# A two-branch mixer block: recurrence units that hold two pairs of heads over 256 tokens, and a GpSimd queue in written order under the attention

## The chip, the cores and the metric

One core of one Trainium2 chip. The metric is the device time of one execution in microseconds (us); of several runs the median is taken.

## What is computed

One block with 1024 tokens of width 1024, all in fp32: a modulated RMS norm, a mixer of two branches (causal attention with a forget gate, 8 heads of 64; a delta-rule recurrence, 8 heads of 64), a gated merge, an output projection, and a feed-forward part with a short convolution. The change touches the two branches only:

```python
# recurrence, one step per token and head; state is 64 x 64
sa = einsum('bhvk,bhk->bhv', state, a_t)
state = state * w_t[:, :, None, :] + sa[..., None] * b_t[:, :, None, :] + v_t[..., None] * k_t[:, :, None, :]
y_t = einsum('bhvk,bhk->bhv', state, r_t)
# attention, per block of 128 queries
logits = einsum('bhqd,bhkd->bhqk', q, k) * scale + cum_q - cum_k     # cum: sums of the log forget gates
probs = softmax(where(causal, logits, -inf))
out = einsum('bhqk,bhkd->bhqd', probs, v)
```

## The kernel before, in words

**Order of the work.** TensorE's instructions stand in an order that the program writes itself (`manual_schedule`, L139). A planner, `Weave` (L48), keeps a model time `now`, advanced by a modelled cost for each matmul (`mm_cost`, L67). Work that has latency runs as chains (Python generators); a chain yields the time after which it wants to go on. While no chain is due, `fill` (L104) lets the next matmuls of a queue of projections run: items of `weave.first`, then of `weave.queue`. An item in progress is finished first, and one further item has had its weights loaded already, so a new item in `weave.first` starts behind both. An item that sets `weave.hold` stops the filling until that time. Except where a part of the program is marked as written order, the other engines' orders are made by a scheduler.

**Fill.** The projections of the recurrence's inputs `rkv_items` (L387; 24 halves of 24 matmuls of 128x512), of the attention's q and k (`qk_steps`, L400), of v (`v_steps`, L1032) and of 16 gates (`gate_steps`, L336; two halves of 24 matmuls each). Gates left at the attention's start run as its fill (`late_gate`, L1306, on the bank `rk_ps`), and what is left at its end runs behind it.

**Recurrence.** It is worked in chunks of 64 tokens. A unit is one pair of heads (128 rows: two heads of 64) over 512 tokens, that is 8 chunks; there are 4 pairs and 2 halves of the tokens, 8 units. Two chains run side by side:

- `pre` (L814) of unit k: decays, normalized keys and the scaled operands on VectorE and ScalarE (per-channel factors such as `V("k_k", p)` differ by pair); the chunks' matrices `E` by matmuls `p`; a round trip of their 32x32 blocks through DRAM (`sm`, `M32`) for `inverse` (L787), 62 small VectorE instructions, and back (`se`, `TT`); transposes and the bonus term. `ready` is the time at which the planner takes `TT` to have landed. `pre` of unit k waits until unit k-2 has passed two points of `main` (`passed`).
- `main` (L924) of unit k: VectorE transposes `X` out of `TT` (planned at `ready` less 1500 ns), then matmuls `xi`, `zi`, `uw`, `mz`, then the state's steps. A step per chunk: `sp` += Mt times S0 (one matmul for each of the two heads, each issued to TensorE as two instructions), VectorE scales it by the chunk's decay to the next state S (L996), `yp` += S0 times Zt. Between steps the chain yields 1150 ns, and the fill's matmuls come between. At the end come two head sums (`mu`, `va`), the normalization, and the store of the output to `d_orw`.

The tiles for r, k and v have one buffer for each half of the tokens; the items for the next pair are put into `weave.first` when `pre` of a unit is done, and `pre_chain` (L1058) runs the fill itself until a unit's inputs are there.

**Attention.** Three chains: logits (`s_chain`, L1122), transposes of the probabilities (`t_chain`, L1208), products with v (`a_chain`, L1251). VectorE and ScalarE are in written order here (L1109), GpSimd is not. GpSimd issues the loads of each head (`load_head`, L1093: `stA` of 1 MB, `stB` of 0.5 MB, `vh` of 0.5 MB, two buffers each), multiplies the outputs by the inverse sums and splits them into `fx` (`collect`, L1271). The inverse sums go through DRAM: ScalarE issues the store `d_rs` and, 3.5 us of plan later, the load `R` that spreads them over 64 rows (`spread`, L1194). The outputs' tile `o` has two buffers. ScalarE's table for Exp and Tanh is asked for at L1340, the table for Ln and Exp in `use_ln_exp` (L203).

Of the kernel before, what the change touches and what calls it, by code (L numbers as in the profile page):

```python
# [16 lines left out]
S = 1024  # L17
# [17 lines left out]
NVEC = _n  # L35
NOSYNC = mybir.DependencyInfo(mybir.DependencyClass.NoSync, mybir.DependencyReason.DATA)
# [99 lines left out]
def hybrid_block(ctx: ExitStack, tc: tile.TileContext, a, out):  # L136
# [66 lines left out]
    def use_ln_exp(after=None):  # L203

        i = nc.scalar.preload_act_table_set("natural_log_exp_and_others")
        if after is not None:
            tc.add_manual_dep(i.ins, after.ins.name, NOSYNC)
# [128 lines left out]
    def gate_steps(w, i, pps, ptag, pool, tag):  # L336
        if weave.late == 1:
            yield from late_gate(w, i)
            return
        for hf in range(2):  # L340
            cs = slice(hf * NH, hf * NH + NH)
            ps = pps.tile([128, NH], F32, tag=ptag, name=f"gt{i}_{hf}")
            yield from gemm_steps(ps, w[0:2], u, cs)

            g = pool.tile([128, NH], F32, tag=tag, name=f"gs{i}_{hf}")
            if weave.late:
                nc.scalar.activation(g, ps, AF.Tanh, scale=0.5)
# [6 lines left out]
            stt(g, ps, 0.0, g, op0=ALU.min, op1=ALU.subtract)  # L354
            nc.scalar.activation(g, g, AF.Exp)
            nc.sync.dma_start(d_gate[i, :, cs], g)
# [3 lines left out]
    with ExitStack() as es:  # L360
# [26 lines left out]
        def rkv_items(p, hf):  # L387
            ts_ = {x: rkp.tile([128, NH], F32, tag=f"{x}{hf}", name=f"{x}{p}{hf}") for x in "rkv"}
            rkv[p, hf], got[p, hf] = [ts_[x] for x in "rkv"], 0

            def steps(w, x, t):
                if hf == 0:
                    last_col[p, x] = shp.tile([128, 1], F32, tag=f"pv{x}", name=f"pv{p}{x}")
                yield from shifted(w, t, hf, ts_[x], last_col[p, x], f"rkv{t}")
                got[p, hf] += 1

            for x, t in (("k", 4 + p), ("r", p), ("v", 8 + p)):
                yield (lambda t=t: w_in(12 + t)), (lambda w, x=x, t=t: steps(w, x, t))
# [253 lines left out]
        with tc.tile_pool(name="lg", bufs=1, reuse_waits="tile") as lg, \  # L652
# [47 lines left out]
            def lora_chain():  # L700
# [11 lines left out]
                while got[0, 0] < 3:  # L712
                    weave.step()
# [48 lines left out]
            weave.first.extend([*rkv_items(0, 0), *rkv_items(0, 1)])  # L762
# [7 lines left out]
        def hx(ap, x):  # L770
            return ap.rearrange("p (c x) -> p c x", x=x)

# [14 lines left out]
        def inverse(n, M32, TT, chunk_tile, tmp):  # L787
# [3 lines left out]
            t32 = tmp("t32", 256)  # L791
# [22 lines left out]
        def pre(k, p, hf):  # L814

            n = f"{p}_{hf}"
            cs = slice(hf * NH, hf * NH + NH)
            rr, kk, vv = rkv[p, hf]
# [8 lines left out]
            nc.sync.dma_start(cum, d_lora[0, p, :, cs])  # L827
            al = tmp("al")
            nc.sync.dma_start(al, d_lora[1, p, :, cs])
            ksq = tmp("ksq")  # L830
            nc.scalar.activation(ksq, kk, AF.Square, scale=V("k_k", p))
            parts = rw.tile([128, 3, NH], F32R, tag="bk", name=f"kp{n}")
            yield 1275 if p + hf else 6000
# [12 lines left out]
            stt(kr, rn, 1e12, kk, op0=ALU.min, op1=ALU.mult)  # L846
# [4 lines left out]
            stt(ar[:, 0], c3(kr), nkk[:, p : p + 1], el[:, :, 0:CH], op0=ALU.mult, op1=ALU.mult)  # L851
# [3 lines left out]
            tt(ar[:, 1], c3(rr), el[:, :, 1:], op=ALU.mult)  # L855
            ts(al, al, V("k_a", p), oka[:, p : p + 1], op0=ALU.mult, op1=ALU.add)
            tt(al, al, kk, op=ALU.mult)
            tt(bk[:, :, 1, :], c3(al), c3(en), op=ALU.mult)
            pcd = chunk_tile("pcd", 3, NCU)
            nc.gpsimd.tensor_copy(pcd, el[:, :, CH])  # L860
            rkb = tmp("ksq")
            stt(rkb, rr, V("r_k", p), al, op0=ALU.mult, op1=ALU.mult)
# [26 lines left out]
            for g in range(4):  # L889
                nc.sync.dma_start(M32[g * 32 : g * 32 + 32, :, :], sm.rearrange("h c b s t -> (h c b) s t"))  # L890
            ready = weave.now + (47500 if k == 0 else 38500)
            TT = chunk_tile("TT", 2, NCU, CH)
            weave.spawn(inverse(n, M32, TT, chunk_tile, tmp), 8500)

            vt, at = gen(f"vt{n}"), gen(f"at{n}")
            for b in range(4):
                bs = slice(b * 128, b * 128 + 128)
                transpose(vt[:, bs], vv[:, bs], ident)
                transpose(at[:, bs], ar[:, 0, 2 * b : 2 * b + 2, :], ident)
# [21 lines left out]
            tt(bon, bp, vv, op=ALU.mult)  # L921
            units[p, hf] = dict(ready=ready, pcd=pcd, ar=ar, E=E, QA=QA, TT=TT, bon=bon, UV=UV)

        def main(k, p, hf):  # L924
            o = units.pop((p, hf))
            n = f"{p}_{hf}"
            cs = slice(hf * NH, hf * NH + NH)
# [52 lines left out]
            S0 = state.get(p)  # L980

            for c in range(NCU):
                alone = hf == 0 and c == 0
                for h in range(2):
                    mm(sp[HS[h], c, :], E[:, c, h, 2, :], UV[:, c, h, :], start=c == 0, stop=alone, more=True)
                for h in range(2):
                    mm(yp[HS[h], c, :], UV[:, c, h, :], E[:, c, h, 1, :], start=c == 0, stop=alone, more=True)
            yield 2400
            for c in range(NCU):
                if S0 is not None:  # L990
                    for h in range(2):
                        mm(sp[HS[h], c, :], Mt[HS[h], c, :], S0[HS[h], :], start=False, stop=True, more=True)
                S1 = None
                if not (hf == 1 and c == NCU - 1):
                    S1 = rw.tile([128, CH], F32, tag="state", name=f"S{n}{c}", bufs=3)
                    ts(S1, sp[:, c, :], pcd[:, c : c + 1], None, op0=ALU.mult)  # L996
                if S0 is not None:
                    for h in range(2):
                        mm(yp[HS[h], c, :], S0[HS[h], :], Zt[HS[h], c, :], start=False, stop=True, more=True)
                if c + 1 < NCU:  # L1000
                    yield 1150
                S0 = state[p] = S1
# [19 lines left out]
            nc.scalar.activation(rs, rs, AF.Exp, scale=-0.5)  # L1022
            stt(y, y, V("ln_w", p), rs, op0=ALU.mult, op1=ALU.mult)
            stt(y, y, V("ln_b", p), bon, op0=ALU.add, op1=ALU.add)
            gg = rw.tile([128, NH], F32, tag="Wt", name=f"gg{n}", bufs=1)
            nc.sync.dma_start(gg, d_lora[2, p, :, cs])
            ov = rw.tile([128, NH], F32, tag="ysq", name=f"o{n}", bufs=1)
            tt(ov, y, gg, op=ALU.mult)
            nc.sync.dma_start(d_orw[p, :, cs], ov)
# [25 lines left out]
        order = [(p, hf) for p in range(4) for hf in range(2)]  # L1055
        passed.update((k, x) for k in (-1, -2) for x in range(2))

        def pre_chain():  # L1058
            for k, (p, hf) in enumerate(order):
                while got[p, hf] < 3:  # L1060
                    weave.step()
                yield from pre(k, p, hf)
                if p < 3:
                    weave.first.extend(rkv_items(p + 1, hf))
                yield 0

        def main_chain():
            for k, (p, hf) in enumerate(order):
                while (p, hf) not in units:
                    yield 200  # L1070
                yield from main(k, p, hf)
# [11 lines left out]
    heads = {}  # L1083

    def load_first():
# [5 lines left out]
        heads[0] = *tiles[0:4], tiles[4].rearrange("p (a x) -> p a x", x=128)  # L1091

    def load_head(h):  # L1093
        A = at.tile([128, 2, S], F32R, tag="stA", name=f"stA{h}")
        nc.gpsimd.dma_start(A, d_st[h, 0:2, :, :].rearrange("k r s -> r k s"))
        B = at.tile([128, 2, S], F32R, tag="stB", name=f"stB{h}")
        nc.gpsimd.dma_start(B[0:68, :, :], d_st[h, 2:4, 0:68, :].rearrange("k r s -> r k s"))
        vh = at.tile([128, 8, 128], F32R, tag="vh", name=f"vh{h}")
        nc.gpsimd.dma_start(vh, d_v[h])
        heads[h] = A[:, 0, :], A[:, 1, :], B[:, 0, :], B[:, 1, :], vh  # L1100

    load_first()
    while len(weave.queue) > 12:
# [5 lines left out]
    with tc.manual_schedule(engines={mybir.EngineType.DVE, mybir.EngineType.Activation}):  # L1109
# [12 lines left out]
        def s_chain():  # L1122

            yield 3500
            for k, (h, I) in enumerate(seq):
                if k % 4 == 1 and h < 7:
                    load_head(h + 1)
                qa, ka, qb, kb, _ = heads[h]
# [19 lines left out]
        def softmax(h, rows, lgt):  # L1148
# [17 lines left out]
            for i, n, nm, lg in part:  # L1166
                e = (at.tile([128, S], F32, tag="P", name=f"P{h}_{i}", bufs=4) if i > 3 else
# [26 lines left out]
        def spread(h, hf, tp):  # L1194
            p = h // 2
            rt = at.tile([4, 128], F32, tag="rt", name=f"rt{h}_{hf}", bufs=1)
# [7 lines left out]
            nc.scalar.dma_start(norms[p, hf][h % 2 * 64 : h % 2 * 64 + 64, :],  # L1204
# [45 lines left out]

        def a_chain():  # L1251

            for _ in range(8 * 10):
# [6 lines left out]
                vh = heads[h][4]  # L1260
# [5 lines left out]
                th_free.append(weave.now + 260)  # L1266
                if jj == I:
# [72 lines left out]
        nc.scalar.preload_act_table_set("exp_and_others")  # L1340
# [28 lines left out]
    def br_open(x, n):  # L1369
# [5 lines left out]
        nc.scalar.copy(hi, raw)  # L1375
# [9 lines left out]
    use_ln_exp(marks["gate"])  # L1385
# [754 lines left out]
```

## Time and profile before

| | |
|---|---|
| median of 3 runs | 1646.33 us (1641.17 to 1647.93) |
| the profiled execution | 1646.9 us, span 1645.1 us |
| mean granted TensorE clock | 0.991 |

| stretch (us from the span's start) | what runs there |
|---|---|
| 0 to 136 | norm, low-rank projections, modulation |
| 136 to 612 | the recurrence with its fill |
| 612 to 812 | the attention with its fill |
| 812 to 899 | the branches' output projections (`br`) |
| 899 to 1645 | output projection and feed-forward part |

How to read it: a busy row counts an engine's instructions, the column in brackets says what ended the idle time before an instruction and how long it was. Matmuls overlap, so the cost of one in a series is the distance from start to start and not its own duration. `f32 x8` at the end of a row of the timeline are eight instructions in a row that were merged.

### The profile page before, as it was taken

The numbers are of one execution on the slowest core, as the hardware profiler recorded it, in microseconds if no ns is written. First come the engines' busy times: TensorE is split into PE (matmuls) and PEld (weight loads), VectorE is DVE, ScalarE is ACT, GpSimd is POOL, SyncE is SP. The second block draws the span as 40 slices with busy tenths as digits, with TensorE's granted clock in tenths as the row PEclk, the third lists the DMA queues.
The fourth block names the chain that finished last, engine by engine and source line by source line (L and its number), as shares of the span: only waits on it lengthen the run. The fifth ranks groups of instructions, "written<-read, shape, count | busy, mean of one in ns | idle before, by whom it ended". The sixth has DMA issues, their size and how long they took to land.

```text
span 1645.1 us, 25963 instructions
## 1 busy us (share of the span) xinstructions
PE 1614.0 (98%) x9756; PEld 1327.9 (81%) x9756; DVE 1197.2 (73%) x2334; ACT 808.4 (49%) x1473; POOL 139.7 (8%) x169
## 2 busy tenths in 40 slices
PE   7999999999999999999999999999999999999998
PEld 5777877887887778788888888888888888888886
DVE  6875887887876636777579346887777777786677
ACT  7663434443455546676524135644444444555455
POOL 0011101211111020222132000000000000000000
PEclk8999999999999999999999999999999999999999
DMA  9587644543343236543487310242332232675363
GB/s 346 185 314 228 166 129 122 136 121 91 111 119 89 89 107 179 135 136 106 148 322 259 135 65 27 83 135 96 104 114 96 96 109 97 223 256 160 122 211 109
DMA packets 123902, 241.72 MB, mean 147 GB/s; under 512 B 39816, under 2 KB 48320, under 8 KB 123776
## 3 DMA queue, kind: packets, MB, share of 16 engines
q1 hardware_dynamic: 114944, 220.94, 41.3%
q0 software_dynamic: 7600, 17.25, 3.8%
q10 hardware_dynamic: 1232, 1.86, 0.4%
q8 instruction: 77, 1.26, 0.3%
q14 instruction: 49, 0.40, 0.1%
HBM read 174.43 MB, written 65.56 MB: 146 GB/s over the span
## 4 chain that ended last, share of the span: by engine, by line
PE 88%; DVE 6%; ACT 3%; DMA 1%; issue 1%; POOL 0%; SPq 0%; DVEq 0%; ACTq 0%; POOLq 0%
PE X L144 14%; PE D L144 13%; PE Y L144 6%; PE gt L144 6%; PE ps_rkv L144 6%; PE wo L144 5%; PE br L144 5%; PE rk_ps L144 4%; PE qk L144 4%; PE W L144 3%; PE v L144 3%; PE ov L144 2%; PE lg L144 2%; PE tp L151 2%; PE low L144 1%; PE sp L144 1%
## 5 line engine op out<-in xcount | busy, mean ns | idle before, releaser
L144 PE MATMUL D<-op,op 128*128 128x512 f32 x924 | 209.8, 389 | 0.0
L144 PEld LDWEIGHTS D<-op,op 128*128 128x128 f32 x924 | 173.3, 188 | 36.3 <-DVE op L1403 0.3
L144 PE MATMUL X<-T_m,S 128*128 128x512 f32 x440 | 107.3, 390 | 0.1
L144 PEld LDWEIGHTS X<-T_m,S 128*128 128x128 f32 x440 | 82.4, 188 | 18.2 <-ACT T_m L1828 0.6
L1402 ACT CAST op<-g 128x512 fp32r<-128x512 f32 x77 | 47.8, 621 | 73.0 <-PE D L144 48.1
L1403 DVE TENSOR_TENSOR op<-g,op 128x512 fp32r<-128x512 f32 x77 | 53.0, 688 | 41.3 <-ACT op L1402 41.3
L1639 DVE SCALAR_TENSOR_TENSOR c<-ab,vec,c 128x512 f32<-128x512 f32 x88 | 65.9, 749 | 19.5 <-ACT c L1642 17.9
L1603 DVE TENSOR_TENSOR S<-ur,S 128x512 fp32r<-128x512 f32 x66 | 45.5, 691 | 35.6 <-ACT S L1599 35.5
L1246 DVE TENSOR_TENSOR tl<-tp,th 128x512 fp32r<-128x512 f32 (+1 forms) x80 | 49.9, 633 | 28.0 <-ACT th L1238 24.5
L270 DVE TENSOR_TENSOR lo_in<-raw_in,hi_in 128x512 fp32r<-128x512 f32 x84 | 57.9, 728 | 15.9 <-PE gt L144 7.7
L1599 ACT CAST S<-ur 128x512 fp32r<-128x512 f32 x66 | 41.0, 622 | 55.6 <-DVE ur L1592 30.6
L1603 DVE TENSOR_TENSOR A<-ur,A 128x512 fp32r<-128x512 f32 x64 | 44.0, 688 | 30.9 <-ACT A L1599 30.7
L266 ACT CAST hi_in<-raw_in 128x1024 fp32r<-128x1024 f32 x42 | 43.9, 1048 | 45.2 <-PE ps_rkv L144 28.0
L144 PE MATMUL Y<-T_h,A 128*128 128x512 f32 x264 | 63.5, 389 | 0.0
L795 DVE TENSOR_TENSOR t<-E,M 128x60 f32<-128x60 f32 (+24 forms) x248 | 54.8, 221 | 11.8 <-DMA M<-sm 5.7
L144 PE MATMUL Y<-T_h,S 128*128 128x512 f32 x264 | 63.3, 389 | 0.0
L799 DVE TENSOR_TENSOR E<-E,t 128x60 f32<-128x60 f32 (+24 forms) x248 | 57.9, 234 | 5.8
L144 PE MATMUL X<-B_b,A 128*128 128x512 f32 x252 | 60.8, 390 | 0.0
L144 PE MATMUL W<-B_f,A 128*128 128x512 f32 x252 | 60.6, 389 | 0.0
L1238 ACT CAST th<-tp 128x512 fp32r<-128x512 f32 (+1 forms) x80 | 42.4, 542 | 33.7 <-PE tp L151 31.3
L144 PEld LDWEIGHTS Y<-T_h,A 128*128 128x128 f32 x264 | 49.5, 188 | 10.4
L144 PEld LDWEIGHTS Y<-T_h,S 128*128 128x128 f32 x264 | 49.5, 188 | 10.3
(494 smaller groups left out, 4071.6 us busy)
## 6 DMA issues: line engine op xcount, KB each, us to landing
raw_in<-in_w_in SPq DMA_DIRECT2D x50, 512.0 KB
wm<-in_w_mod SPq DMA_DIRECT2D x48, 512.0 KB
ur<-in_w_up SPq DMA_DIRECT2D x44, 512.0 KB
g<-d_g SPq DMA_DIRECT2D x35, 512.0 KB
d_g<-gs SPq DMA_DIRECT2D x44, 256.0 KB
d_g<-c SPq DMA_DIRECT2D x33, 256.0 KB
d_st<-qh SPq DMA_DIRECT2D x64, 128.0 KB
d_gate<-gs SPq DMA_DIRECT2D x32, 256.0 KB
```

The lines of the kernel that those rows point to most:

```text
L144: weave.last = nc.tensor.matmul(o, lhsT, rhs, start=start, stop=stop, skip_group_check=more)
L266: i = nc.scalar.copy(hi, raw)
L270: nc.vector.tensor_tensor(lo[:, c : c + NH], raw[:, c : c + NH], f32(hi[:, c : c + NH]), op=ALU.subtract)
L795: i = tt(tv, E32[:, 0:J, s : s + 1].to_broadcast([128, J, W]), M32[:, s : s + 1, s + 1 : 32].to_broadcast([128, J, W]), op=ALU.mult)
L799: tt(E32[:, 0:J, s + 1 : 32], E32[:, 0:J, s + 1 : 32], tv, op=ALU.add)
L1238: nc.scalar.copy(th[:, 0:w], tp[:, 0:w])
L1246: tt(tl[:, 0:w], tp[:, 0:w], f32(th[:, 0:w]), op=ALU.subtract)
L1402: nc.scalar.copy(hi, src)
L1403: tt(lo, src, f32(hi), op=ALU.subtract)
L1599: nc.scalar.copy(hi, src)
L1603: tt(lo, src, f32(hi), op=ALU.subtract)
L1639: stt(c, ab[:, x + hf * NH : x + hf * NH + NH], V("conv_w", 22 * x + i), c, op0=ALU.mult, op1=ALU.add)
```

## The change

The recurrence's unit becomes two pairs of heads (a group g, with j = 0, 1) over 256 tokens (a quarter), still 8 chunks in a unit and 8 units. Chunk 4*j + i of a unit is chunk i of pair j, so a unit has 4 steps of the state in place of 8, each for both pairs. Operations with per-channel factors are split into two of 256 columns. Loads and stores of `d_lora` and `d_orw` cover two pairs by 256 columns.

```diff
         def rkv_items(g, hf, x):
             def steps(w, p, t):
+                if p % 2 == 0:
+                    while x not in free:
+                        weave.hold = weave.now + 200
+                        yield
+                    free.remove(x)
+                    rkv[g, hf, x] = rkp.tile([128, 2, NH], F32, tag=x, name=f"{x}{g}{hf}")
...
-            stt(kr, kr, V("k_k", p), al, op0=ALU.mult, op1=ALU.mult)
+            for j, p in pairs:
+                stt(j2(kr)[:, j], j2(kr)[:, j], V("k_k", p), j2(al)[:, j], op0=ALU.mult, op1=ALU.mult)
...
-            ready = weave.now + (47500 if k == 0 else 38500)
+            ready = weave.now + (47500 if k == 0 else 50000)
...
+            if not odd and (g, hf) != (1, 1):
+                for x in "krv":
+                    weave.first.extend(rkv_items(*((g, 1) if hf == 0 else (g + 1, 0)), x))
+            yield from arrived("v")
...
-            for c in range(NCU):
+            for i in range(4):
                 if S0 is not None:
-                    for h in range(2):
-                        mm(sp[HS[h], c, :], Mt[HS[h], c, :], S0[HS[h], :], start=False, stop=True, more=True)
+                    for j in range(2):
+                        for h in range(2):
+                            mm(sp[HS[h], 4 * j + i, :], Mt[HS[h], 4 * j + i, :], S0[HS[h], j, :], start=False, stop=True, more=True)
...
-                    ts(S1, sp[:, c, :], pcd[:, c : c + 1], None, op0=ALU.mult)
+                    tt(S1, sp[:, i::4, :], pcd[:, i::4].unsqueeze(2).to_broadcast([128, 2, CH]), op=ALU.mult)
...
-                if c + 1 < NCU:
-                    yield 1150
+                if i < 3:
+                    yield 1300
```

The tiles for r, k and v now have one buffer each, of two pairs by 512 tokens; a name is in `free` again when `pre` of an odd quarter has read it for the last time. The items for the next 512 tokens are put into `weave.first` in `pre` of an even quarter, behind its matmuls `p`; `pre` itself waits for its inputs by `arrived`, which polls every 200 ns while the other chains go on, in place of the loop in `pre_chain` that ran the fill.

In the attention GpSimd is in written order too; heads' loads carry a wait for the last TensorE instruction that was written before them; `vh` is loaded apart from `stA` and `stB`; head 1 is loaded before the attention's start; the load `R` is issued by GpSimd in place of ScalarE; `o` has three buffers, `rt` two; the probabilities of the four longer rows have a tile each.

```diff
+    def fetch(dst, src):
+        i = nc.gpsimd.dma_start(dst, src)
+        tc.add_manual_dep(i.ins, weave.last.ins.name, SYNC)
...
-    with tc.manual_schedule(engines={mybir.EngineType.DVE, mybir.EngineType.Activation}):
+    with tc.manual_schedule(engines={mybir.EngineType.Pool, mybir.EngineType.DVE, mybir.EngineType.Activation}):
...
-                if k % 4 == 1 and h < 7:
-                    load_head(h + 1)
+                if k % 4 == 1 and 0 < h < 7:
+                    load_head(h + 1, fetch)
+                if k in (2, 4):
+                    load_v(k // 2)
...
-            nc.scalar.dma_start(norms[p, hf][h % 2 * 64 : h % 2 * 64 + 64, :],
+            nc.gpsimd.dma_start(norms[p, hf][h % 2 * 64 : h % 2 * 64 + 64, :],
...
+                ends[h] = ends.get(h, 0) + 1
+                if ends[h] == 10 and 0 < h < 6:
+                    load_v(h + 2)
...
-                halves[p, hf] = at.tile([128, NH], F32, tag="o", name=f"o{p}{hf}"), []
+                halves[p, hf] = at.tile([128, NH], F32, tag="o", name=f"o{p}{hf}", bufs=3), []
```

Both table loads get an order: the one for Exp and Tanh behind the last Exp of an early gate (`early`) and of the recurrence (`rs`), the one for Ln and Exp behind the last gate and a copy of a branch's weights (`hi`).

```diff
-        nc.scalar.preload_act_table_set("exp_and_others")
+        table = nc.scalar.preload_act_table_set("exp_and_others")
+        for x in ("early", "rs"):
+            tc.add_manual_dep(table.ins, marks[x].ins.name, NOSYNC)
...
-    use_ln_exp(marks["gate"])
+    use_ln_exp(marks["gate"], marks["hi"])
```

More of the change, by code (lines that the diff above doesn't have):

```diff
@@ L711, in lora_chain @@
                 mod_out(5)
-                while got[0, 0] < 3:
+                while min(got.get((0, 0, x), 0) for x in "krv") < 2:
                     weave.step()
@@ L979, in main @@
             sp = py.tile([128, NCU, CH], F32, tag="sp", name=f"sp{n}")
-            S0 = state.get(p)
+            S0 = state.get(g)
             for c in range(NCU):
-                alone = hf == 0 and c == 0
+                alone = quarter == 0 and c % 4 == 0
                 for h in range(2):
@@ L1053, in hybrid_block @@
             weave.add(lambda i=i: w_in(26 + i), lambda w, i=i: gate_steps(w, i, pb, "big", gsp, "sp0"))
-        order = [(p, hf) for p in range(4) for hf in range(2)]
+        order = [(g, quarter) for g in range(2) for quarter in range(4)]
         passed.update((k, x) for k in (-1, -2) for x in range(2))
         def pre_chain():
[L1059 to L1064, printed above, removed]
+            for k, o in enumerate(order):
+                yield from pre(k, *o)
                 yield 0
         def main_chain():
-            for k, (p, hf) in enumerate(order):
-                while (p, hf) not in units:
+            for k, o in enumerate(order):
+                while k not in units:
                     yield 200
-                yield from main(k, p, hf)
+                yield from main(k, *o)
                 yield 0
@@ L1249, in halve @@
             av_queue.append((t + 210, h, I, jj, th, tl))
+        ends = {}
         def a_chain():
```

157 lines of the change are left out of this document (97 added, 60 removed).

## The prediction

> **What bounds the kernel now.** I read the page first, then the busy times by stage, then what TensorE waited for.
>
> ```profile
> span 1645.1 us, 25963 instructions
> PE 1614.0 (98%) x9756; PEld 1327.9 (81%) x9756; DVE 1197.2 (73%) x2334; ACT 808.4 (49%) x1473; POOL 139.7 (8%) x169
> ```
>
> TensorE (PE) is busy for 1614.0 of 1645.1 us. The 31 us of gaps are all that a shorter wait anywhere could give back; more must come from matmuls that get cheaper. The stages that the change touches, and the one group of gaps in the attention that is of any size, by columns of length, PE, weight loads, VectorE (DVE), ScalarE (ACT), GpSimd (POOL) and the granted clock:
>
> ```profile
> 266.00:314.00 48.00, 47.62 (x478) 36.83 (x473) 40.51 (x116) 21.20 (x39) 8.85 (x11) 1.00 0.55 141
> 612.00:812.00 200.00, 193.23 (x1169) 169.34 (x1168) 142.09 (x273) 131.12 (x299) 44.05 (x60) 0.98 0.46 131
> 682.00:692.00 10.00, 6.94 (x24) 5.73 (x23) 4.52 (x8) 3.80 (x11) 1.23 (x2) 0.66 0.71 194
> ```
>
> ```profile
> PE lg L144 <- ACT P L1173: 3.9, 4, 3.1
> PE rk_ps L144 <- ACT gs L1325: 2.5, 4, 1.2
> PE sp L144 <- DVE S L996: 1.0, 3, 0.4
> ```
>
> The first row is one unit of the recurrence: 48 us, PE without gaps, VectorE 84% busy. The state's chain, eight steps one after the other, makes PE wait 1.0 us in all (third row of the waits), because the fill covers it. So a shorter chain by itself gives nothing; it only moves fill to a later place. In the attention PE idles 6.8 of 200 us, 3.1 of them in one place, where the clock falls as well (0.66 over 10 us).
>
> **The change part by part. 1. The state's steps.** The timeline of PE in the last unit shows one visit to the state between two stretches of fill; then the pace of fill alone; then a long series of matmuls of the same 64x64 shape; last, both groups over the whole recurrence.
>
> ```profile
> 586.81 0.33 PE L144 MATMUL sp<-S,Mt 64*64 64x64 f32 x4
> 586.98 0.28 PE L144 MATMUL yp<-Zt,S 64*64 64x64 f32 x4
> 587.19 1.65 PE L144 MATMUL gt<-u_hi,lo_in 128*128 128x512 f32 x6
> 588.77 0.33 PE L144 MATMUL sp<-S,Mt 64*64 64x64 f32 x4
> ```
> ```profile
> 605.72 1.98 PE L144 MATMUL gt<-u_lo,hi_in 128*128 128x512 f32 x8
> 607.53 1.98 PE L144 MATMUL gt<-u_hi,lo_in 128*128 128x512 f32 x8
> ```
> ```profile
> 313.40 1.15 PE L144 MATMUL q<-UV,E 64*64 64x64 f32 x32
> 314.47 0.69 PE L144 MATMUL xi<-X,E 32*32 32x32 f32 x32
> ```
> ```profile
> L144 PE MATMUL sp<-S,Mt 64*64 64x64 f32 x240 | 19.9, 242 | 1.3 <-DVE S L996 1.0
> L144 PE MATMUL yp<-Zt,S 64*64 64x64 f32 x240 | 17.0, 218 | 0.0
> ```
>
> From one visit to the next are 588.77 - 586.81 = 1.96 us. Six fill matmuls take 6 x (607.53 - 605.72)/8 = 6 x 0.226 = 1.36 us, so a visit of 8 small matmuls costs 0.60 us. In a series 32 of that shape take 314.47 - 313.40 = 1.07 us, 0.033 each, 0.27 for eight. The other 0.33 us is paid for each visit, for going from fill to the state and back. There are 240/4 = 60 visits (60 x 0.60 = 36 us; the groups show 19.9 + 17.0 = 36.9). The change makes them 30 (8 units of 4 steps, less the two first steps of the two groups, which have no state), of 16 matmuls each: the matmuls are the same 480. Saved are 30 x 0.33 = 9.9 us, and as PE is the bound with no gaps here, they come off the time.
>
> The Trainium skill ("TensorEngine Tiling (Array Packing)", Key Properties) says that changing the tiling mode, between 128x128 fill and 64x64 state work here, drains TensorE; by that rule the cost goes with the visits, as I have it. The same page (Instruction Overhead) says that each matmul carries about 60 cycles; by that rule the cost goes with the matmuls, none of which go, and this term would be 0. The rows speak for the first, 0.075 us for a matmul in a visit against 0.033 in a series.
>
> Bounds: 0, if all of the 0.60 goes with the matmuls, and 30 x 0.60 = 18, if none does; I take 9.9, which both rows give.
>
> **2. The stop in the attention at 685 us.** ACT, GpSimd and PE around it:
>
> ```profile
> 683.26 0.36 ACT L1277 COPY o<-ov 64x256 f32<-64x256 f32 x1 [4.65 <-POOL fx L1296]
> ```
> ```profile
> 677.53 1.43 POOL L1290 TENSOR_TENSOR o<-o,R 128x256 f32<-128x256 f32 x2 [2.71 <-DMA R<-d_rs]
> 679.58 0.76 POOL L1095 DMA_DIRECT2D stA<-d_st  x1
> 680.34 1.00 POOL L1097 DMA_DIRECT2D stB<-d_st  x1
> 681.36 1.87 POOL L1296 TENSOR_TENSOR fx<-o,fx 128x256 fp32r<-128x256 f32 x2
> ```
> ```profile
> 677.47 0.40 PE L144 MATMUL lg<-stB 68*128 68x512 f32 x1
> 677.71 0.40 PE L144 MATMUL lg<-stA 128*128 128x512 f32 x1
> 685.40 0.79 PE L144 MATMUL lg<-stA 128*128 128x512 f32 x1 [3.06 <-ACT P L1173]
> 685.99 0.63 PE L144 MATMUL lg<-stB 68*128 68x512 f32 x1
> 686.41 0.63 PE L144 MATMUL lg<-stA 128*128 128x512 f32 x1
> ```
>
> ACT wants a new `o`; both buffers are taken until GpSimd's last read (L1296), which stood behind the wait for `R` and two load issues. ACT, in written order, held the next Exp, and PE stopped for 3.06 us. Then a logits matmul takes 686.41 - 685.99 = 0.42 us where it took 677.71 - 677.47 = 0.24: the clock is down for about 6 us (685.4 to 691.4), which costs 6 x (1 - 0.24/0.42) = 2.6 us. A third `o` takes away the wait for the buffer; the loads' issues (1.8 us here) come at the plan's places. Gain 3.1 + 2.6 = 5.7 us; bounds 0 and, with all of the 6.8 us of gaps, 9.4. I take 5.7, since this one wait is named by its row.
>
> What is added: 14 issues of `R` move from ACT to GpSimd. By GpSimd's issue rows they cost 0.4 to 1.0 us each, 6 to 14 us beside 44 busy of 200; behind each stand the multiplications by `R`, the `fx` splits and the next loads, and for `fx` nobody waits before the next stage. The new wait of `stA` and `stB` for PE stops GpSimd until the planned place; behind it stand the same. I take 0 here and put the case that loads come late among the rivals. `vh` no longer sits behind `stB`.
>
> **3. The table load.**
>
> ```profile
> 618.14 0.63 ACT L355 ACTIVATE gs<-gs 128x512 f32<-128x512 f32 x1 [0.76 <-DVE gs L354]
> 621.64 1.01 ACT L1173 ACTIVATE P<-lg,nm 128x896 f32<-128x896 f32 x1 [2.87 <-DVE nm L1162]
> 622.76 1.28 ACT L1325 ACT_TABLE_LOAD   x1
> 624.70 2.14 PE L144 MATMUL rk_ps<-u_hi,hi_in 128*128 128x512 f32 x8 [1.18 <-ACT gs L1325]
> ```
>
> The load of 1.28 us stands ahead of the first Tanh, and the fill waits 1.18 us for that. Ordered behind the last early Exp (618.14), it falls into the 2.87 us in which ACT is idle anyway. Gain 1.2 us; bounds 0 and 1.2. The order at the other end only keeps a load where it is: 0.
>
> **4. VectorE's instructions.**
>
> ```profile
> L996 DVE TENSOR_SCALAR S<-sp,pcd 128x64 f32<-128x64 f32 x8 | 2.2, 279 | 3.7 <-PE sp L144 3.7
> L974 DVE TENSOR_TENSOR Zt<-mz,ar 128x256 f32<-128x256 f32 x2 | 0.8, 421 | 0.2 <-PE mz L144 0.2
> L862 DVE SCALAR_TENSOR_TENSOR ksq<-r,vec,al 128x512 f32<-128x512 f32 x1 | 0.7, 745 | 0.0
> ```
>
> Six instructions of 512 columns in each unit become twelve of 256: 48 x (2 x 0.42 - 0.745) = 4.6 us more. 60 scalings of the state (60 x 0.279 = 16.7) become 30 of 128 columns, each between 0.279 and 0.42: 4 to 8 us less. Together about 0, hidden behind PE; without that cover a few us at most.
>
> **5. Where the fill goes.** By the plan a unit yields 8 x 1150 - 1150 = 8050 ns between steps before and 3 x 1300 = 3900 after, so eight units end 33 us earlier by the plan and take less fill. The gates that are left run in the attention and behind it:
>
> ```profile
> L144 PE MATMUL rk_ps<-u_lo,hi_in 128*128 128x512 f32 x112 | 32.6, 402 | 0.0
> ```
>
> (8 such matmuls for a half: 112/8 = 14 halves, 7 of 16 gates; 2 to 3 more would be left.) PE's work is the same, so 0; the cover is that PE has fill everywhere. It has none where `weave.hold` stops it: an item for k may find its buffer not yet free. In a plan of these lengths that can happen once, when the items of the second group come in: they are put in when unit 0 is through, the buffer is free when unit 1 has passed `mz`, about 30 us later, and before them go the rest of the item in progress and one whole item of 48 x 0.226 = 10.8 us. As fill has about 60% of PE here (478 instructions in the row of 266 to 314, some 350 of them the recurrence's, leave 130 x 0.226 = 29 of 48 us), that covers 18 to 36 of the 30 us. A stop of 0 to 12 us, with own work for 40% of it, costs 0 to 7 us; with the slower clock after it up to 10. I take 3.
>
> **The sum**, against the profiled execution's 1646.9 us: -9.9 - 5.7 - 1.2 + 3 = -13.8, that is 1633.1. The median of the runs shown is 0.6 lower, so I say 1632.5 us.
>
> **The rivals.** (a) The cost goes with the matmuls and not with the visits: term 1 is 0, and the time is 1642.4. For it speaks the rule above, against it the two rows of small matmuls. (b) `TT` comes late and VectorE, which takes its instructions in order, stands still in each unit, so that PE runs out of evacuated banks. It happened once in the trace:
>
> ```profile
> 214.21 0.43 DVE L936 STREAM_TRANSPOSE X<-TT 32x256 f32<-32x256 f32 x1 [3.84 <-DMA TT<-se]
> 216.19 1.20 PE L144 MATMUL qk<-u_hi,hi_in 128*128 128x512 f32 x4 [2.26 <-DVE v L383]
> ```
>
> Its price is 2.26 us of PE and about 2 of slower clock. For it: VectorE has 40.5 of 48 us in a unit, and the unit gets about 6 us shorter (four visits less of 1.96, longer ones in their place), so its 62 small instructions for `inverse` are squeezed. Against it: `ready` is put 11.5 us later, which gives `TT` that much more time with fill beside it. Seven units at 4.3 us are 30 us: 1662; it decides from five units on (1632.5 + 22 = 1654, 0.5% slower than before). (c) GpSimd in written order stands waiting for `R` (2.71 us in the row above) and for the multiplications when a head's load is due, and the logits of the next head wait. `stB` needs long:
>
> ```profile
> stB<-d_st POOLq DMA_DIRECT2D x7, 544.0 KB, 12.3
> ```
>
> A head lasts 200/8 = 25 us and the load is written a quarter into it, so about 18 us ahead: a delay of over 6 us at GpSimd reaches PE. Every second head has such multiplications at its start: three stops like the one at 685 us, 3 x 5.7 = 17 us, in place of term 2's gain: 1632.5 + 17 = 1649.6, no change. (d) The stop at 685 us returns elsewhere in the attention and the table's 1.2 is all that the second part brings: 1638.2.
>
> **How the numbers follow.** Forecast 60%, (a) 10%, (b) 12%, (c) 9%, (d) 9%. The forecast's own range goes from 1646.3 - 18 - 9.4 - 1.2 = 1618 by all favourable bounds to 1640 with term 5 at 10; I cut the low end to 1622, since 18 and 9.4 can hardly come together. Holding (a), (c) and (d) takes the high end to 1650; left out are (b) and the low tail, together under 2 in 10. A measurement of this kernel can't tell 0.5%, 8 us, from no change: faster is below 1638, which the forecast reaches mostly and (d) in half: 0.67. Same holds (a), (c), half of (d) and the forecast's upper part: 0.20. Slower is (b), and a little of (c): 0.13.
>
> **What would show it right or wrong.** Right: `sp<-S,Mt` and `yp<-Zt,S` still x240 each, in 30 visits of 8 + 8, the sum of both groups near 30 x 0.87 = 26 us in place of 36.9; no stop of ACT at `o` behind GpSimd; a table load ahead of the first `P`; more than 14 halves as late gates. Wrong: a visit that costs 1.2 us (a); `X<-TT` with waits in several units (b); `lg<-stB` or `lg<-stA` behind a DMA (c); PE gaps over 5 us between 250 and 300 us, with no fill (term 5).

## The result and the profile after

Of six runs each, the changed kernel takes 1660.46 us (1659.22 to 1661.29) and the kernel before 1643.08 us (1640.32 to 1647.93): a ratio of 1.0102, 95% interval 1.0085 to 1.0119. The change makes the kernel slower by 1%. I had said 1632.5 us, with 0.13 for slower.

The head of the page after:

```profile
span 1658.6 us, 26003 instructions
PE 1610.6 (97%) x9756; PEld 1330.4 (80%) x9756; DVE 1203.2 (73%) x2354; ACT 809.3 (49%) x1484; POOL 144.7 (9%) x183
```

TensorE's busy time fell by 3.4 us, but its gaps grew from 31 to 48 us. Where they lie is read from three marks: the first late gate (`rk_ps`), which opens the attention, its number of matmuls, and the first `br`, which ends it. First the kernel before, then after (first and last start stand ahead of the semicolon):

```profile
L144 PE MATMUL rk_ps<-u_hi,hi_in x112: 387/395/504, 615.3 to 807.6; 128*128 128x512 f32 x112
L144 PE MATMUL br<-fx,hi_br x128: 389/389/389, 811.5 to 853.8; 128*128 128x512 f32 x128
```
```profile
L145 PE MATMUL rk_ps<-u_hi,hi_in x96: 387/396/628, 621.4 to 801.4; 128*128 128x512 f32 x96
L145 PE MATMUL br<-fx,hi_br x128: 387/389/628, 823.4 to 867.5; 128*128 128x512 f32 x128
```

Eight of these matmuls belong to a gate half, so before there were 14 late halves and now there are 12: two more were done in the recurrence. A half is 24 matmuls at the 0.226 us that the prediction takes from a series, 5.43 us. Up to the first `rk_ps` the changed kernel is 6.1 us later but has done 10.9 us more fill: a gain of 4.8. The attention takes 202.0 us with 12 halves against 196.2 with 14: a loss of 5.8 + 10.9 = 16.7. From `br` to the end it is 835.2 against 833.6, a loss of 1.6. Together 13.5, the difference of the spans.

In the recurrence (130 to 640 us) the groups of the state's steps:

```profile
L145 PE MATMUL sp<-S,Mt 64*64 64x64 f32 x240 | 13.4, 230 | 3.6 <-DVE S L1048 3.2 <-DVE sh_rkv L378 0.4
L145 PE MATMUL yp<-Zt,S 64*64 64x64 f32 x240 | 12.0, 218 | 0.0
```

25.4 us in place of 36.9: the same 480 matmuls cost 11.5 us less in half as many visits. Measured from start to start in the seventh unit, a visit of 16 takes 0.84 us (2.42 us from 551.31 to 553.73, less seven fill matmuls at 0.226). But `sp` now waits 3.2 us for VectorE's `S`, and others in the same stretch wait as well:

```profile
PE zi L145 <- ACT X L994: 2.2, 1, 2.2
PE rk_ps L145 <- ACT gs L1391: 1.8, 1, 1.8
PE at L152 <- DVE E L923: 1.3, 1, 1.3
PE gt L145 <- DVE gs L355: 1.0, 1, 1.0
```

In the attention (600 to 850 us) the waits, and the stretches in which the granted clock (third column from the right) fell:

```profile
PE lg L145 <- DMA stB<-d_st: 9.7, 3, 4.7
...
PE br L145 <- issue: 2.1, 1, 2.1
PE ov L145 <- DVE o L1345: 1.4, 1, 1.4
```
```profile
712.00:722.00 10.00, 8.70 (x41) 0.68 0.11 38
...
752.00:762.00 10.00, 4.95 (x31) 0.86 0.68 133
762.00:772.00 10.00, 10.00 (x51) 0.80 0.20 58
...
812.00:832.00 20.00, 16.67 (x77) 0.83 0.53 183
```

The stop behind `o` is gone, and another has come twice: the logits wait for the DMA that brings `stB`. After each the clock is low, and again at the end of the attention, where no late gate is left to cover a wait. By 1 less the clock, these rows lose 3.2, 1.4 + 2.0 and 3.4 us. The place of the first stop, GpSimd's queue and then TensorE:

```profile
689.44 0.54 POOL L1265 DMA_DIRECT2D R<-d_rs  x1
693.59 1.43 POOL L1356 TENSOR_TENSOR o<-o,R 128x256 f32<-128x256 f32 x2 [3.61 <-DMA R<-d_rs]
695.09 0.61 POOL L1359 CAST fx<-o 128x512 fp32r<-128x512 f32 x1
695.77 1.44 POOL L1362 TENSOR_TENSOR fx<-o,fx 128x256 fp32r<-128x256 f32 x2
697.16 0.76 POOL L1146 DMA_DIRECT2D stA<-d_st  x1
697.91 1.01 POOL L1146 DMA_DIRECT2D stB<-d_st  x1
```
```profile
708.55 0.48 PE L145 MATMUL lg<-stA 128*128 128x512 f32 x1
713.30 0.79 PE L145 MATMUL lg<-stB 68*128 68x512 f32 x1 [4.28 <-DMA stB<-d_st]
```

The loads of head 4 stand in the queue behind `o` and `fx` of the first pair, and `o` waits for `R`, which GpSimd now issues itself. `stB` goes out at 697.9 and is used at 713.3, 15.4 us later; `stA`, issued just before it, was there in time. In the kernel before, the same load went out at 680.3 (the row quoted in the prediction), in an attention that began 6.1 us earlier. The whole attention's landings after, by DMA group (600 to 830 us):

```profile
stB<-d_st POOLq DMA_DIRECT2D x7, 544.0 KB, 14.4
vh<-d_v POOLq DMA_DIRECT2D x7, 512.0 KB, 14.5
R<-d_rs POOLq DMA_DIRECT2D x14, 128.0 KB, 10.8
```

### The profile page after: what moved, and what is told of

It is laid out like the page before. It is cut to its first block, busy times and chain, and to the rows that moved or that the text cites. A ratio compares the mean times of both kernels' runs of the same rounds, so it can differ in the third digit from the quotient of the medians.

```text
span 1658.6 us, 26003 instructions
## 1 busy us (share of the span) xinstructions
PE 1610.6 (97%) x9756; PEld 1330.4 (80%) x9756; DVE 1203.2 (73%) x2354; ACT 809.3 (49%) x1484; POOL 144.7 (9%) x183
## 4 chain that ended last, share of the span: by engine, by line
PE 59%; DMA 4%; DVE 3%; ACT 2%; POOL 1%; issue 1%; SPq 0%; POOLq 0%; ACTq 0%
PE X L145 13%; PE D L145 13%; PE Y L145 6%; PE wo L145 5%; PE br L145 5%; PE gt L145 4%; PE W L145 3%; DMA stB<-d_st 3%; PE rk_ps L145 2%; PE ov L145 1%; PE lg L145 1%; PE tp L152 1%; PE tr L145 1%; DMA d_gate<-gs 1%; DMA R<-d_rs 0%
## 5 line engine op out<-in xcount | busy, mean ns | idle before, releaser
L816 DVE TENSOR_TENSOR t<-E,M 128x60 f32<-128x60 f32 (+24 forms) x248 | 59.3, 239 | 20.6 <-DMA M<-sm 7.5
```

What stands on the lines that cost most here:

```text
L816: i = tt(tv, E32[:, 0:J, s : s + 1].to_broadcast([128, J, W]), M32[:, s : s + 1, s + 1 : 32].to_broadcast([128, J, W]), op=ALU.mult)
```

## The experiments

My theory after this (A in the expectations): most of the loss is the lateness of two heads' `stB`, so GpSimd's new order and waits, which I took at 0, are the failed step. The rivals: the recurrence is what costs, because it ends with less fill in hand (B), or the removed stop was worth nothing. Ratios are to the kernel before, with 95% intervals.

| run | what it is | median us | ratio |
|---|---|---|---|
| after | the change | 1660.46 | 1.0102 (1.0085 to 1.0119) |
| e1_rec_only | its recurrence part | 1657.9 | 1.0079 (1.0055 to 1.0104) |
| e2_att_only | its attention part | 1656.37 | 1.0078 (1.0053 to 1.0103) |
| e3_load_sooner | after, heads' loads a quarter sooner | 1646.12 | 1.0013 (0.9997 to 1.0029) |
| e4_split_stB | after, `stB` as 64 + 4 rows | 1643.24 | 1.0004 (0.9991 to 1.0017) |
| e13_loads_free | after, GpSimd unordered, loads without wait | 1647.68 | 1.0027 (1.0014 to 1.0039) |
| e6_R_on_act | after, `R` issued by ScalarE | 1653.25 | 1.006 (1.0041 to 1.008) |
| e10_att_split | e2 with `stB` split | 1638.69 | 0.9967 (0.9955 to 0.998) |
| e11_before_split | before with `stB` split | 1643.91 | 1.0006 (0.9993 to 1.0018) |
| e8b_o3 | before with three `o` | 1640.28 | 0.9989 (0.9978 to 0.9999) |
| e12_rec_v | e1, values' second item later | 1650.51 | 1.0042 (1.0027 to 1.0057) |
| e9_split_v | e4, values' second item later | 1638.57 | 0.9974 (0.996 to 0.9988) |
| e7_ready | after, 38.5 us in place of 50 | 1687.8 | 1.0268 (1.0252 to 1.0285) |
| e14_all | e9 with 38.5 us | 1675.66 | 1.02 (1.0181 to 1.0218) |

### Which part costs: e1_rec_only, e2_att_only

e1 takes over the part of the diff up to the end of the recurrence, with the attention as before; e2 takes over the rest.

> Only the recurrence's part of the change; the attention, its loads and its queues as before. Theory A (the loss is made by the late head loads of the attention): the recurrence part alone gains about 5 us by the attention's start, of which the attention may give back up to 5 because two halves of a gate fewer are left as fill: 1638 to 1643 us beside 1643 before. Theory B (the loss is made by the recurrence, which takes a gate more of the fill so that the attention's end has none): about 7 us slower than before, 1650.

> Only the attention's part of the change (GpSimd in written order, loads by the plan, R on GpSimd, three o, ordered tables); the recurrence as before. Theory A: stops at stB of 4 to 5 us twice, with 3 us of slower clock behind each, less the 5.7 us of the old stop: about 10 us slower than before, 1653. Theory B: with the old recurrence's 14 halves of late gates there is fill, the old stop is gone: about 5 us faster, 1638.

Each part alone costs about 13 us, and both together 17: they don't add. e1 is above both of its expectations and e2 above that of A. e2 shows the two late `stB` with the old recurrence:

```profile
PE lg L145 <- DMA stB<-d_st: 11.0, 2, 6.1
```

e1 has no late load. It loses at both ends of the attention:

```profile
PE rk_ps L145 <- ACT gs L1376: 6.6, 4, 5.2
PE lg L145 <- ACT P L1224: 2.5, 3, 1.9
PE ov L145 <- ACT th L1289: 2.2, 1, 2.2
PE br L145 <- issue: 2.1, 1, 2.1
```

The first row is ScalarE waiting for the store of an early gate ahead of the first late one:

```profile
635.40 1.28 ACT L1376 ACT_TABLE_LOAD   x1 [4.07 <-DMA d_gate<-gs]
```

The last two are an attention whose 12 late halves were used up. So both the theory and the first rival hold a part.

### The late loads: e3_load_sooner, e4_split_stB, e13_loads_free, e6_R_on_act

```diff
-                if k % 4 == 1 and 0 < h < 7:      # e3
+                if k % 4 == 0 and 0 < h < 7:
```
```diff
-        fetch(B[0:68, :, :], d_st[h, 2:4, 0:68, :].rearrange("k r s -> r k s"))      # e4
+        fetch(B[0:64, :, :], d_st[h, 2:4, 0:64, :].rearrange("k r s -> r k s"))
+        fetch(B[64:68, :, :], d_st[h, 2:4, 64:68, :].rearrange("k r s -> r k s"))
```
```diff
-        i = nc.gpsimd.dma_start(dst, src)      # e13, and Pool out of manual_schedule
-        tc.add_manual_dep(i.ins, weave.last.ins.name, SYNC)
+        nc.gpsimd.dma_start(dst, src)
```
```diff
-            nc.gpsimd.dma_start(norms[p, hf][h % 2 * 64 : h % 2 * 64 + 64, :],      # e6
+            nc.scalar.dma_start(norms[p, hf][h % 2 * 64 : h % 2 * 64 + 64, :],
```

> The changed kernel with the load of head h+1 written at the first of the four steps of head h in place of the second, about 6 us sooner. Theory A: the stops at stB (9.7 us and some 6 of slower clock) go, 1644 to 1647 against 1660. Theory B: nothing changes by more than 3 us.

> The changed kernel with stB loaded as 64 rows and 4 rows in place of 68 rows. If stB lands 14 us after its issue because 68 rows are spread over few DMA engines, the 64 rows land some 5 us sooner, the stops at stB go in part, and the time falls by 5 to 12 us; if it lands late because it stands behind stA and the other loads of the same queue, it lands at 13 to 15 us as before and the time stays within 3 us of 1660.

> The changed kernel with GpSimd not in written order and the heads' loads without their wait for TensorE; the loads still stand where the plan emits them. The late stB are those of heads 4 and 6, whose loads wait in the changed kernel not for TensorE but behind o and fx, which wait for R. If that place in the queue is the cause, the loads of heads 3, 5 and 7 go out sooner here, those of heads 4 and 6 at most a few us sooner, one or both stops stay, and the time is within 5 us of the changed kernel's (ratio to before 1.006 to 1.010). If the written order and the added wait are the cause, both stops go and the ratio is 1.001.

> The changed kernel with the loads of R given back to ScalarE's queue. On GpSimd's queue an R takes 10.8 us to land behind stA and stB, and o waits 3.3 to 3.6 us for it with the loads of heads 4 and 6 behind it. If R is what holds those loads up, they go out 3 us sooner or more, the 9.7 us of waits for stB fall below 3 us and the ratio to before falls to about 1.001. If the loads are late because of where they stand and of the 14 us that the stB take, the waits stay above 6 us and the ratio stays at 1.006 or above.

e4 moves nothing in the order and takes away 16 us, more than the 5 to 12 that I had expected. Its landings in the attention, against the 14.4 above:

```profile
stB<-d_st POOLq DMA_DIRECT2D x7, 512.0 KB, 8.5
...
stB<-d_st POOLq DMA_DIRECT2D x7, 32.0 KB, 8.7
```

TensorE doesn't wait for `stB` at all. With the same 12 late halves the attention takes 182.9 us (621.1 to 804.0) where the changed kernel takes 202.0. Not all of these 19.1 us are the two long stops: at the logits ahead of them e4 is already 4.4 us in front (`lg` at 681.63 against 686.07), mainly because TensorE waits at most 0.6 us for a late gate in place of 1.8 and the clock from 630 to 640 us is 1.00 in place of 0.83. Nor is a shorter landing all that the split changes. `R` behind it on the same queue lands in 4.8 us in place of 10.8, and head 4's `stB` goes out at 691.3 in place of 697.9; e4 does not part these. e3 does nearly the same by time alone: `stB` of head 4 goes out at 690.1, and 1.8 us of waits for `stB` are left. Either brings the load some 6 to 8 us forward, and that is enough for stops of 4.3 and 4.7 us.

e13 refutes what I had said of it. I held the place behind `o` and `fx` to be the cause and expected a stop to stay; none did. Its row for GpSimd shows why:

```profile
689.98 0.77 POOL L1146 DMA_DIRECT2D stA<-d_st  x1 [0.44 <-PE lg L145]
690.77 1.44 POOL L1361 TENSOR_TENSOR fx<-o,fx 128x256 fp32r<-128x256 f32 x2
692.15 1.03 POOL L1146 DMA_DIRECT2D stB<-d_st  x1
```

With the odd heads' loads no longer held for TensorE, `R` landed sooner (3.7 us in place of 10.8), `o` went through sooner, and head 4's `stB` was out 5.8 us earlier than in the changed kernel, though TensorE was 2.8 us behind there (the same `lg` at 688.83). So the written order and the wait for TensorE do cost, 12 us together, by way of transfers that run into each other; no run takes away one of the two alone. What e13 still lacks against e4 is the wait that e1 has: 4.3 us at `gs`, behind the store of a gate. It issues head 2's loads at 617 us, as the kernel before does; e4 and after issue them at about 650.

e6 came out between its two cases: 3.4 us of waits for `stB` are left of 9.7, and the ratio is 1.006. Head 4's load goes out only 1.1 us sooner (696.9), and now waits for TensorE. `R` is a part of the cause, not the whole.

### What the removed stop is worth: e8b_o3, e10_att_split, e11_before_split

A third `o` alone (e8_o3) gave no time: with it the attention's buffers need 82.75 KB in a partition, where 81 are left. e8b therefore also cuts the four large `P` to their rows' sizes, as the change does.

```diff
-                halves[p, hf] = at.tile([128, NH], F32, tag="o", name=f"o{p}{hf}"), []      # e8b, and P by sizes
+                halves[p, hf] = at.tile([128, NH], F32, tag="o", name=f"o{p}{hf}", bufs=3), []
```

> The kernel before with three buffers for the attention output o, and the four large P buffers cut to the sizes that the changed kernel uses (same number of buffers in the same turn, which makes the room). If the stop at 685 us is a cost of its own, it goes: 3.06 us of idle TensorE and 2.6 us of lower clock, 5.7 us in all, ratio 0.9965. If the wait only passes to what stands behind it, the ratio stays between 0.999 and 1.001.

> The attention part of the change alone (recurrence as before), with stB loaded as 64 rows and 4 rows instead of 68. If the late stB landings (11.0 us of waits and the lower clock behind them) were all that the attention part cost, this run shows what it gains when they are gone: the stop at 685 us (5.7) and the table load (1.2), so about 6 us below the kernel before, ratio 0.996. If GpSimd in written order costs something else too, the ratio stays at 1.0 or above.

> The kernel before with stB loaded as 64 rows and 4 rows. It has no wait for stB, so if the split only cures late landings, the ratio is 1.000 (within 0.0015). If the 68-row load costs something else (DMA engines that the weights or the other loads then miss), the time falls by 2 us or more.

e8b's ScalarE no longer waits at `o`, and TensorE's wait for `P` goes from 3.9 to 0.9 us:

```profile
PE lg L144 <- ACT P L1173: 0.9, 3, 0.5
```

The time falls by 1.8 us (0.2 to 3.6), not by 5.7; the ratio lies between my two cases, at the edge of the second. In e11, which keeps two `o`, the same wait is 2.2 us in all and 1.3 at most; in e1 and e12, which keep them too, it is at most 1.9 and 2.9. The profiled execution of the kernel before had a long one, 3.1 us, and I took it for all of them. e10 is 5.4 us faster than the kernel before (3.3 to 7.4), as expected of it; e11 shows that the split adds nothing to a kernel without late loads. So the attention part is worth about 5 us once its loads come in time, and e10 beats both kernels.

### Why the recurrence gives nothing: e12_rec_v, e9_split_v, e7_ready, e14_all

In the changed kernel the last `xi` stands at 573.8 us against 566.5 before, and from the sixth unit to the seventh it takes 72 us (460.6 to 532.4) where the others take 41 to 54. The inputs of the second group's second half stood behind both items of attention's values, 37 us each. e9 and e12 put a gate between the two:

```diff
-        for j in range(2):
-            weave.add(lambda j=j: [load_w(a["w_v"][j, x], f"v{j}{x}") for x in range(2)], lambda w, j=j: v_steps(w, j))
         for i in range(16):
+            if i < 2:
+                weave.add(lambda j=i: [load_w(a["w_v"][j, x], f"v{j}{x}") for x in range(2)], lambda w, j=i: v_steps(w, j))
             weave.add(lambda i=i: w_in(26 + i), lambda w, i=i: gate_steps(w, i, pb, "big", gsp, "sp0"))
```

and e7 and e14 put the planned time before a unit's main part back from 50000 to 38500.

> The recurrence part of the change alone, with the second item of attention's values behind the first gate item. The recurrence part alone cost 13 us. If that came of a recurrence that ended late with 20 gate halves done, so that attention ran out of fill at its end (2.2 and 2.1 us of waits, granted clock 0.85 from 802 to 822), this run has 14 halves left there, the stops at the end are gone, and the ratio falls from 1.008 to about 1.003 or below. If the cost is the stop at 637 us (ScalarE behind a gate's store, 5.2 us, clock 0.66) and that comes of the new recurrence as such, the ratio stays at 1.006 or above.

> The changed kernel with stB split, and with the second of the two 37 us fill items of attention's values set behind the first gate item instead of directly behind the first. If the recurrence lost its lead because the inputs of the second group's second half stood behind both of those items, the step from the sixth to the seventh unit (72 us, xi at 460.6 and 532.4) falls to about 45 to 50 us, the recurrence ends with at least two fewer gate halves done, attention has 14 or more left and doesn't run out of fill at its end: 5 to 8 us below the changed kernel with the split alone, ratio to before 0.996. If the step is set by VectorE's inverse and not by the inputs, it stays above 65 us and the ratio stays at 1.000.

> The changed kernel with one number put back: a unit's main part may begin 38.5 us after its products instead of 50 us. In the changed kernel VectorE never waits for the inverse (X<-TT stands 0.3 us idle), so for most units the plan's 50 us sets when the main part begins, about 60 us from p to xi. If that number sets the pace of the recurrence, the units come sooner (p to xi about 50 to 55 us, the last xi before 560 us instead of 573), one or two gate halves fewer are done in it, and the time falls by 3 to 6 us (ratio to before 1.006 to 1.008; the late stB stay). If the inverse and VectorE set the pace, xi doesn't come sooner, X waits for TT's landing by some us, and the ratio stays at 1.010 or above.

> The changed kernel with stB split, the second item of attention's values behind the first gate item, and 38.5 us instead of 50 us. With stB split and the order alone the ratio was 0.9974. If the pace of the units is the plan's 50 us, the recurrence ends sooner with the same work, TensorE keeps more fill for attention, and the ratio falls to 0.995 or below. If the new recurrence is held by VectorE and the inverse, TensorE waits for X and TT instead, and the ratio stays between 0.997 and 1.000: then the 11.5 us that the state steps save on TensorE are worth nothing here.

e9 gains about 5 us on e4, the low end of what was expected, though its step from the sixth unit to the seventh is 59 us (466.8 to 526.1) and not 45 to 50. It has 14 late halves, and the end of the attention is covered: first e4, whose last late matmuls start at 789.6 us, then e9.

```profile
792.00:802.00 10.00, 7.42 (x52) 1.00 0.07 28
802.00:812.00 10.00, 7.99 (x28) 0.83 0.92 326
```
```profile
792.00:802.00 10.00, 10.00 (x68) 1.00 0.00 0
802.00:812.00 10.00, 10.00 (x46) 1.00 0.85 283
```

e12 falls from 1.0079 to 1.0042, not quite to the 1.003: the place of that item is about half of what the recurrence part costs alone, and the stop ahead of the first late gate stays (3.4 us).

e7 says what the 50 us are for. With 38.5 the changed kernel loses another 27 us:

```profile
PE xi L145 <- DVE X L987: 27.0, 8, 10.1
```
```profile
L987 DVE STREAM_TRANSPOSE X<-TT 32x256 f32<-32x256 f32 x16 | 6.9, 432 | 18.8 <-DMA TT<-se 18.6
```

In the changed kernel the second group is idle for 0.3 us. TensorE, in written order, stands at `xi` until `TT` has landed and VectorE has transposed it. The last `xi` comes at 606.0 us, later than the 573.8 with 50. So the way from `p` over `inverse` to `TT` holds the units back here, not the state's steps, and the planned 50 us keeps TensorE from standing there. e14 shows the same without late loads (36.5 us at `xi`); its ratio of 1.02 lies outside both cases that I had expected.

With the same attention and late loads repaired, the new recurrence (e9) stands at 0.9974 and the old one (e10) at 0.9967, and the intervals overlap. The 11.5 us that the visits save aren't seen in the time. (e9's profiled execution took 1644.5 us, well above its median; e10's 1639.3.)

## Why the prediction was wrong, step by step

**The state's steps (-9.9): the price was right, that it comes off the time was not.** The saving is 11.5 us, 0.38 for each visit saved where I had 0.33, and rival (a) is out: the matmuls are the same 480. That the cost goes with the visits agrees with the Trainium skill's rule ("TensorEngine Tiling (Array Packing)", Key Properties) that a change of the tiling mode drains TensorE; what a visit spends the time on, no run shows. But "as PE is the bound with no gaps here, they come off the time" failed: the waits for `S`, `X`, `E` and `gs` came in, and 4.8 us were left up to the attention. I had also taken 8 us for too little to tell from no change; the interval of these six runs is 2.8 us to each side.

**Where the fill goes (+3): the fill went the other way, and the loss was of another kind.** I let the units end 33 us earlier by the plan and have 2 to 3 more late halves. The last unit's `xi` came 7 us later, and two fewer were left. I had counted the shorter yields between steps and passed over what the 50 us do: by the plan the 11.5 us added to `ready` outweigh the 4.15 us by which a unit's steps get shorter, and `inverse` needs that time (e7). The two halves themselves were lost to the place of the values' second item: with the same 50 us, e9 and e12 have 14. The stop by `weave.hold` that I priced between 250 and 300 us didn't come: that row has 1.9 us of gaps. What I had not priced is fill that is missing at the end of the attention, about 5 us by e4 against e9; that 3 and 5 are near each other is luck.

**The stop at 685 us (-5.7): mechanism right, size wrong.** The stop went. It is worth 1.8 us (0.2 to 3.6) by itself; the whole attention part with loads in time is worth 5.4.

**The new order and waits on GpSimd (0): the failed step.** It is rival (c), to which I gave 9%, and its mechanism is what the traces show: `o` waits 3.6 us for `R`, the load of head 4 (and 6) behind it goes out late, and the logits stop. I had reckoned with 18 us from issue to use and a landing of 12.3; head 4's `stB` had 15.4, and the landings took 14.4 at the median (11.2 to 18.5). I had three stops at 5.7 us, 17 in all; there were two long ones of 4.3 and 4.7 us with 6.6 us of slower clock behind them, 15.6, and e4 without them is 16 us faster. That the totals lie so near is luck. That (c) came out at 1649.6, no change, is the sum around it: with 4.8 us for the steps in place of 9.9 and nothing for the table it would have been 1655.9, slower.

**The table load (-1.2): moved as said, gained nothing in the changed kernel.** It stands at 624.90, ahead of the first `P`. The first late gate then waited 1.8 us all the same, for a store that held its buffer:

```profile
624.90 1.28 ACT L1406 ACT_TABLE_LOAD   x1
...
630.80 0.60 ACT L1391 ACTIVATE gs<-rk_ps 128x512 f32<-128x512 f32 x1 [1.95 <-DMA d_gate<-gs]
```

**VectorE's instructions (0).** Its busy time rose by 6.0 us over the whole kernel (1197.2 to 1203.2); no run moves these instructions alone.

**Rival (b)** (`TT` late, VectorE stands still) did not come in the changed kernel. e7, without the longer `ready`, costs 27 us where (b) had 30, but by another wait: TensorE stands at `xi` itself and not for evacuated banks.

What stays open: why ScalarE waits over 4 us for a gate's store at the attention's start in e1 and e13, about 2 in e12 and after, and 0.4 in e4. e1 and e13 issue head 2's loads right behind head 1's (617 to 619 us) and after holds them back to 652, but e12 has them early too, and no run moved that alone. And what takes the rest of the saving in e9, whose waits in the recurrence are some 7 us longer than those of e10, was not split further.

## What to carry to other kernels

An order written by hand is also an order of the transfers: of each load that is moved behind other work, compare the time from its issue to its first use with its measured landing time, place by place, before it is priced at 0. Time saved on the bounding engine in a stage whose pace another chain sets can turn into waits or into fill done early, and the latter is lost if a later stage then lacks that fill. A stop read from one profiled execution is one sample; look for it in a second trace before it goes into the sum.

## What the runs showed of the hardware that I had not expected

**While a load of 68 rows is waited for, few of the DMA engines are busy.** While the changed kernel waits for `stB`, the busy share of the 16 DMA engines (second column from the right) stays at about 0.3, a quarter to a third:

```profile
707.00:709.00 2.00, 2.00 (x14) 1.00 0.32 83
709.00:711.00 2.00, 0.03 (x1) 1.00 0.32 74
711.00:713.00 2.00, 0.00 (x0) 0.62 0.28 82
```

As 64 + 4 rows the same data lands in 8.5 and 8.7 us in place of 14.4, and in the kernel before in 7.4 and 7.5 in place of 12.3. `vh`, of 128 rows, is issued behind it and gains too: 7.2 us in e4 against 14.5 after. The Trainium skill ("DMA: Bandwidth & Descriptors", Why a DMA increments its semaphore by 16 and not by 1) says that a transfer runs on the largest number of engines, up to 16, that divides the slowest dimension on both its sides. By that rule 64 rows get 16 engines and 68 rows 4. The share of 0.3 agrees with that, for 4 engines would be 0.25; it is not of `stB` alone, since `R` and `vh` were issued behind it at 698.9 and 699.5. The same section names an exception for some transfers issued by GpSimd, by which 68 rows would go to 14 engines (an estimate from its rule of rows for each engine); the share does not fit that.
